# A bidirectional RWKV-7 / mLSTM trunk layer: the mLSTM scan in alternating half steps, gate rows computed in the RWKV scan, merge gates in half products, and a fixed TensorE order

## The chip, the cores and the metric

The kernel runs on one core of a Trainium2 chip, as one program. The core has five engines that run side by side: TensorE (PE in the profile; its weight loads are listed apart as PEld), VectorE (DVE), ScalarE (ACT), GpSimd (POOL) and SyncE (SP, which only issues DMAs here). The metric is device time in microseconds, the median of several runs. Everything is computed in float32; large matrix products are made of three products of rounded parts (see below).

## The reference

One layer on 128 context tokens and 1024 latent tokens, width 1024. The latent tokens start each directional scan from a given state; the context tokens start from zero and their final states are outputs.

```python
h = rmsnorm(x, norm_g[0]) * (1 + sc1) + sh1            # sc, sh, g from SiLU(cond) @ ada_w
z_r, z_m, z_g = split(h @ w_in)                        # 1920, 2064 and 2048 columns
y_r, S = rwkv7_bidir(centred_shift(z_r, mu), S0, ...)  # 8 heads of 64, two directions
y_m, (C, n, m) = mlstm_bidir(z_m, C0, n0, m0, ...)     # 4 heads of 128, two directions
gate_r, gate_m = split(sigmoid(z_g))
merged = gate_r * (y_r @ w_branch_rwkv) + gate_m * (y_m @ w_branch_mlstm)
x = x + g1 * rmsnorm(merged @ w_out, norm_g[1])
x = x + g2 * rmsnorm(conv_ffn(rmsnorm(x, norm_g[2]) * (1 + sc2) + sh2), norm_g[3])
```

The mLSTM, for one direction and head, over chunks of tokens (i, f are the log gates; b the running sum of f in the chunk; m the running maximum that keeps the exponentials small):

```python
log_d = where(mask, b[:, None] - b[None, :] + i[None, :], -inf)
m_s   = max(b + m, max(log_d, -1));  inter = exp(b + m - m_s)
s     = (q @ k.T) * exp(log_d - m_s)
num   = inter * (q @ C.T) + s @ v;   den = inter * (q @ n) + sum(s, -1)
h     = num / max(|den|, exp(-m_s))
m_new = max(b[-1] + m, max(b[-1] - b + i));  wj = exp(b[-1] - b + i - m_new)
C, n, m = decay * C + (wj * v).T @ k,  decay * n + wj @ k,  m_new
```

Then the two directions' h are added, normalised per head, scaled and multiplied by sigmoid(o).

## The kernel before

**Layout.** 1152 tokens are nine blocks of 128; block 0 is the context. The normalised input lies transposed in SBUF as AS, three groups of 384 tokens, each as a rounded part and a remainder. `split_w` (L334) loads a weight block, rounds it on ScalarE (L348) and takes the remainder on VectorE (L349); a product is the sum of three products of parts (`mm_split`, L357, its matmul L362).

**Stages in the source.** (1) Modulation, norm and the input projection with everything that prepares the RWKV scan. Its results (KRd, BKd, Vd, Ad ...) and the mLSTM's q, k, v, o and gate columns (qkd, vmd, sod, gtd) go to DRAM. (2) The RWKV scan, 18 steps of 64 tokens (`ORDER`); step n handles one chunk of each direction. (3) The mLSTM, one context chunk and eight latent chunks of 128 tokens in each direction. (4) The merge: branch products, gates (as tanh of half the argument), output projection. (5) The ConvFFN.

**The order within an engine** is not the source's order. The framework takes the source as a list, plans it with a model of the engines' times, and puts each engine's instructions in the order in which they become ready in that plan; dependencies become semaphore waits. An engine works its list in order. Buffers come from rings: the n-th tile of a tag waits until the tile that had its buffer is released.

**The RWKV scan.** `back` (L861) does step n: pP (L867), read out as Pm; pU (L874) into suv; pN (L882) into sn and the next step's suv; pY (L894, L895) into ysum. Between these it calls `between(n)` (L954), which does the next step's scores (`scores`, L813: psc L819, transposes pbk L822, masks L829 and L831), the merge of inverse blocks (`merge`, L836: pmh L843, pmt L852) and `fill(1)`. The loads of the next step (`loads`, L791: KA, BKs, TT on SP, XN on POOL) and of suv (`new_suv`, L761, on POOL) are issued at the step's start. Steps 0 and 1 are the context; after step 1 `finish_ctx` (L906) writes the final states (pfs L910) and `init_state` (L773) loads the latent ones (pst L783), all through the one buffer of tag sn2. `rpost(b)` (L918) finishes an output block: row statistics (L927 to L936), transposes into pgt (L942), pgg (L950), and the store to yrd; `POST` says after which step.

**Filler.** The gate columns z_g are sixteen blocks of 128 columns, each three groups of 24 matmuls (12 weight-part and k steps are one half). Four blocks lie in the preparation, blocks 4 to 12 are cut into groups by `zg_groups` (L710) and handed out by `fill`: one group per scan step, three in the last step, the rest (`fill(len(zq))`) written behind the mLSTM. Blocks 13 to 15 (`zg(f, pss)`) are written after that, next to the reloading of the branch inputs. Each block ends in a Tanh and a store to sgz.

**The mLSTM.** After the scan, three more `rpost`; then the gate rows: loads of gtd, exponentials, two scans along the tokens per direction, a small exchange through DRAM (red, mpd) for the running maximum over chunks, then Ms, it, dc stored to DRAM and three transposes (gT). `mchunk(d, c, CN)` does one chunk in full: it loads qk and vx and broadcasts of the rows (MI), forms dm in four VectorE operations (L1121), takes Exp (L1123), scales the query part of MI (L1124), forms the scores pmP (L1127) and multiplies them in (L1128), transposes k (pmk L1131), scales it (kw L1134), scales the state (CN2, POOL, L1136), and for each pair of heads pmN (L1143, L1144), den (three operations), hsum, pmC (L1161) and the new state (L1162). The two directions alternate. `mfinish(c)` normalises a chunk whose two directions are done (L1170 to L1179), transposes it (pmf L1184), multiplies by the output gate and stores to ymd; it is written one chunk late. After the context chunk the states go out (co, no) and the latent states come in (cn, nr), through the same tag sqm.

**The reload.** `load_y` (L1246) reads yrd and ymd back through the stage buffers (tag zraw, three of them) and splits them into y2r and y2m (L1250, L1251) for the branch products pbr.

## Time and profile before

| what | us |
|---|---|
| median of 3 runs | 2271.1 |
| lowest, highest run | 2270.51, 2271.61 |
| profiled execution, whole | 2279.22 |
| its span in the profile | 2277.5 |
| scan step 0 to step 17 (first and last Pm) | 638.4, 922.9 |
| first pmN of the mLSTM | 985.2 |
| first pbr of the merge | 1177.5 |
| TensorE clock granted, mean | 0.977 |

Times inside the profile count from the span's start. In rows of windows, the bracket behind a busy time is the number of instructions; in rows of groups, the two numbers behind the bar are total busy us and mean ns of one, then the idle time of the engine ahead of them with what ended it. A timeline row is start, length, engine, line, operation, out<-in, shapes and count; idle time ahead of it stands in square brackets.

### The profile page before, as it was taken

The page shows a single profiled execution, that of the slowest core. Times are in us where ns is not written, and L with a number is a line of the kernel's source. Part 1 is how long each engine was busy: PE and PEld are TensorE (multiplying, and loading weights), DVE is VectorE, ACT ScalarE, POOL GpSimd, SP SyncE. Part 2 cuts the span into 40 slices and gives each one's busy share as a digit, 9 for nine tenths or more (in the row PEclk, how much of TensorE's full clock was granted, in tenths as well). Part 3 has the DMA queues.
Part 4 walks back from the last instruction along what each step waited for, and adds up shares of the span by engine and source line. Part 5 has one row for each costly group of instructions (what it writes and reads, how often), then busy time and mean ns, then how long its engine had stood idle before and what let it go on. Part 6 is the DMA issues. An engine that isn't in the chain of part 4 may idle for free. (4 is left out here: it accounts for less than half of the span.)

```text
span 2277.5 us, 40164 instructions
## 1 busy us (share of the span) xinstructions
PE 2119.8 (93%) x16395; PEld 1945.6 (85%) x16395; DVE 1404.3 (62%) x2310; ACT 832.8 (37%) x1683; POOL 534.6 (23%) x699
## 2 busy tenths in 40 slices
PE   6999998989899998977789999999999999999996
PEld 4998997988878987877688978999999999999995
DVE  3766778879555566546833375736555655576558
ACT  3664646462143445434331143432222222222213
POOL 2000198888622233222302212000000000000004
PEclk9999999999989999989999999999999999999999
DMA  9134444545745655367666542111111111111104
GB/s 263 53 86 123 116 127 109 149 106 135 184 121 139 154 145 135 101 185 216 190 184 206 171 157 84 56 47 47 56 49 45 47 56 53 41 47 56 47 19 166
DMA packets 391416, 254.59 MB, mean 112 GB/s; under 512 B 86305, under 2 KB 368069, under 8 KB 391232
## 3 DMA queue, kind: packets, MB, share of 16 engines
q1 hardware_dynamic: 246864, 144.88, 22.7%
q10 hardware_dynamic: 135840, 88.03, 13.0%
q0 software_dynamic: 8528, 19.10, 3.2%
q8 instruction: 129, 2.11, 0.4%
q14 instruction: 55, 0.45, 0.1%
HBM read 186.73 MB, written 65.23 MB: 111 GB/s over the span
## 5 line engine op out<-in xcount | busy, mean ns | idle before, releaser
L362 PE MATMUL pg<-act,whi 128*128 128x384 f32 x4240 | 816.7, 339 | 4.5 <-ACT zraw L522 4.0
L362 PEld LDWEIGHTS pg<-act,whi 128*128 128x128 f32 x4240 | 740.1, 188 | 19.9 <-ACT zraw L522 4.3
L362 PE MATMUL pg<-act,wlo 128*128 128x384 f32 x2120 | 418.0, 337 | 5.0 <-DVE wlo L349 5.0
L362 PEld LDWEIGHTS pg<-act,wlo 128*128 128x128 f32 x2120 | 371.2, 188 | 8.7 <-DVE wlo L349 5.3
L349 DVE TENSOR_TENSOR wlo<-wraw,whi 128x1024 fp32r<-128x1024 f32 x130 | 164.1, 1264 | 226.6 <-ACT whi L348 226.4
L47 DVE SCALAR_TENSOR_TENSOR ua<-uraw,par,ua 128x945 f32<-128x945 f32 (+2 forms) x176 | 214.6, 1219 | 42.5 <-ACT ua L1392 39.3
L362 PE MATMUL pfd<-whi,f 128*128 128x512 f32 x792 | 227.5, 395 | 6.5 <-DVE facc L1464 6.5
L1466 POOL TENSOR_TENSOR x<-facc,grow 128x512 f32<-128x512 f32 x17 | 24.3, 1454 | 822.7 <-DVE facc L1464 822.7
L348 ACT ACTIVATE whi<-wraw 128x1024 fp32r<-128x1024 f32 x130 | 136.7, 1054 | 173.9 <-PE pg L362 99.6
L362 PEld LDWEIGHTS pfd<-whi,f 128*128 128x128 f32 x792 | 146.4, 188 | 37.2 <-DVE facc L1464 9.1
L1464 DVE TENSOR_TENSOR facc<-pfd,facc 128x512 f32<-128x512 f32 x180 | 121.9, 685 | 52.2 <-PE pfd L362 52.2
L509 POOL TENSOR_TENSOR Lb<-Lb,tmp 96x31 f32<-96x31 f32 (+15 forms) x155 | 130.6, 843 | 12.2
L507 POOL TENSOR_TENSOR tmp<-La,Lb 96x31 f32<-96x31 f32 (+15 forms) x155 | 122.6, 791 | 27.3 <-DMA La<-Ad 15.5
L362 PE MATMUL pfd<-wlo,f 128*128 128x512 f32 x396 | 122.6, 391 | 0.0
L1396 ACT ACTIVATE ua<-ua 128x1152 f32<-128x1152 f32 x22 | 25.7, 1168 | 221.3 <-DVE ua L47 221.2
L1406 ACT ACTIVATE f<-ua 128x384 fp32r<-128x384 f32 x66 | 32.1, 518 | 194.0 <-DVE ua L1405 194.0
L829 DVE TENSOR_TENSOR KA<-psc,msk 64x512 f32<-64x512 f32 x72 | 49.2, 684 | 70.2 <-ACT A L828 68.8
L47 DVE SCALAR_TENSOR_TENSOR qacc<-zraw,par,qacc 128x945 f32<-128x945 f32 (+2 forms) x64 | 85.9, 1342 | 9.3 <-ACT qacc L565 8.8
L1340 PE MATMUL pwo<-whi,act 128*128 128x512 f32 x288 | 90.2, 393 | 1.1 <-ACT whi L348 1.1
L362 PEld LDWEIGHTS pfd<-wlo,f 128*128 128x128 f32 x396 | 74.3, 188 | 16.8
L769 POOL DMA_DIRECT2D suv<-Vd x72 | 42.4, 599 | 152.5 <-DVE sn L887 81.8
L1405 DVE TENSOR_TENSOR ua<-pg,ua 128x384 f32<-128x384 f32 x66 | 34.5, 553 | 69.0 <-PE pg L362 53.4
(383 smaller groups left out, 3227.2 us busy)
## 6 DMA issues: line engine op xcount, KB each, us to landing
wraw<-in_w_in ACTq DMA_DIRECT2D x44, 512.0 KB
wraw<-in_ffn_up ACTq DMA_DIRECT2D x44, 512.0 KB
zraw<-in_ada_w SPq DMA_DIRECT2D x24, 512.0 KB
wraw<-in_ffn_down ACTq DMA_DIRECT2D x22, 512.0 KB
KRd<-KR SPq DMA_DIRECT2D x24, 384.0 KB
sgz<-zraw ACTq DMA_DIRECT2D x16, 576.0 KB
KA<-KRd SPq DMA_DIRECT2D x72, 128.0 KB
BKs<-BKd SPq DMA_DIRECT2D x36, 256.0 KB
```

Of the source, the lines that this page charges most:

```text
L47: v.scalar_tensor_tensor(o, img[:, r0 + i:r1 + i, c0 + j:c1 + j], wt, o, op0=ALU.mult, op1=ALU.add)
L348: s.activation(hi, raw, AF.Copy)
L349: v.tensor_tensor(lo, raw, hi.bitcast(F32), op=ALU.subtract)
L362: pe.matmul(out, wt(hw, k), at(ha, k), start=(i == 0), stop=(i == last))
L507: e.tensor_tensor(t3, L[:, j, i].unsqueeze(2).to_broadcast([NI, n, m]), X[:, j:j + 1, c].to_broadcast([NI, n, m]), op=ALU.mult)
L509: e.tensor_tensor(X[:, i, c], X[:, i, c], t3, op=ALU.subtract)
L769: pdma(suv[r, d, h].rearrange("t x p n -> t x (p n)"), src.unsqueeze(1).to_broadcast([64, 2, 4 * LC]))
L829: v.tensor_tensor(q.KA[orr, :, h, :], sc_[h][orr], msk[orr, d:d + 1, :].to_broadcast([64, 4, 128]), op=ALU.mult)
L1340: pe.matmul(pts[b][q], AS[g][:, ha, k, 128 * o:128 * o + 128], wo2[k][hw][:, 0, 512 * q:512 * q + 512], start=(k == 0 and i == 0), stop=(k ...
L1405: v.tensor_tensor(ua[:, gs], pt, ua[:, gs], op=ALU.mult)
L1406: s.activation(f2[:, 0, gs], ua[:, gs], AF.Copy)
L1464: v.tensor_tensor(acc[:, b, qs], pt, acc[:, b, qs], op=ALU.add)
```

## The change

Six edits, made together.

1. **Order.** `pe` becomes a wrapper. While its switch is on (from the first scan step to the end of the mLSTM), every matmul and transpose is pinned behind the TensorE instruction that was written before it.
2. **Halves.** `zg_groups` becomes a generator that stops after 12 of a group's 24 matmuls and after each group; `fill(n)` takes n halves. All of blocks 4 to 15 go through it. The stage ring has two buffers from the scan to the mLSTM's end and three again after it.
3. **Output blocks.** `rpost` is a generator in two parts, statistics first; the second part runs a step later, between the second direction's scores and pN. Six of the blocks come in steps 11 to 16; blocks 1 and 8 come after the scan with two halves each.
4. **Gate rows.** They move into a generator `gates` of six parts, one per scan step 3 to 8. The factor 128^-0.5 is folded into them.
5. **mLSTM.** `mchunk` is cut into `mload` (three half steps ahead), `mfront` (two ahead) and `mback`. The mask is added on POOL and the offset enters Exp as a bias, one per head; the scores of a chunk are formed once, kept as S and used by both directions; the query part is scaled on POOL; pmN and pmC hold four heads, and den, the state update and hsum are done for all four. PSUM is divided anew.
6. **The loop.** Each half step is mback, parts of two finishes, the front two ahead, and one half of a gate product. The context's states go out and the latent ones come in after the second half step, followed by two halves.

```diff
+    class Ordered:
+        on = False
+        def matmul(self, *a, **k):
+            return self.keep(nc.tensor.matmul(*a, **k))
...
+        def keep(self, i):
+            return tc.keep_in_program_order(i) if self.on else i
+    pe = Ordered()
...
+            for g in range(3):
+                if g == 1 and i + 1 < len(fs):
+                    load(fs[i + 1])
+                pt = psg([128, G3])
+                ops = [(h, k) for h in PARTS for k in range(8)]
+                for n, ((hw, ha), k) in enumerate(ops):
+                    pe.matmul(pt, w2s[f][hw][:, k, :], AS[g][:, ha, k, :], start=(n == 0), stop=(n == 23))
+                    if n == 11:
+                        yield
                 s.activation(sg[:, G3 * g:G3 * g + G3], pt, AF.Tanh, scale=0.5)
+                if g == 2:
+                    adma(sgz[f], sg)
+                yield
     def fill(n):
         for _ in range(n):
-            if zq:
-                i, f, g, run = zq.pop(0)
-                run(i, f, g)
+            next(zq, None)
...
+    zsc.close()
+    zst[0] = pool("zst2", 2, zsc)
...
             scores(n + 1, d, qs[d])
+            if d == 1 and posts:
+                next(posts.pop())
             yield
         m = merge(qs)
         next(m)
-        fill(1)
+        fill(2)
         next(m)
         yield
-    POST = {1: 0, 13: 4, 14: 5, 15: 3, 16: 6, 17: 2}
-    zq = zg_groups(list(range(NZ0, 16 - NZ1)))
+    POST = {1: 0, 11: 4, 12: 5, 13: 3, 14: 6, 15: 2, 16: 7}
+    zq = zg_groups(list(range(NZ0, 16)))
...
+        if 2 < n < 9:
+            next(gate)
         if n in POST:
-            rpost(POST[n])
+            posts.append(rpost(POST[n]))
+            next(posts[-1])
+    for b in (1, 8):
+        r = rpost(b)
+        next(r)
+        fill(2)
+        next(r)
...
+    banks(pg=2, ps=2, pf=2)
+    def mfront(q):
+        d, c = q.d, q.c
+        dm, qi = q.MI[:, 0], q.MI[:, 1]
+        q.vx = mp.tile([128, 4, 130], F32, name="vx", tag="vx", bufs=3)
+        dma(q.vx[:, :, 0:128], vmd[c])
+        gp.memset(q.vx[:, :, 128:129], 1.0)
+        gp.tensor_tensor(dm, dm, mbig[:, d:d + 1, :].to_broadcast([128, 4, 128]), op=ALU.add)
+        for h in range(4):
+            s.activation(dm[:, h, :], dm[:, h, :], AF.Exp, scale=-1.0, bias=cols(gT[0], d, c)[:, h:h + 1])
+        if c not in Ss:
+            pp_ = psf([128, 4, 128], "pmP")
             for h in range(4):
+                pe.matmul(pp_[:, h, :], q.qk[:, 4 + h, :], q.qk[:, h, :], start=True, stop=True)
+            Ss[c] = mp.tile([128, 4, 128], F32, name="S", tag="S", bufs=8)
+            s.activation(Ss[c], pp_, AF.Copy)
...
+        v.tensor_tensor(dm, Ss[c], dm, op=ALU.mult)
+        gp.tensor_tensor(qi, q.qk[:, 0:4, :], qi, op=ALU.mult)
...
+    CNs = state(False)
+    qs = [mload(*dc) for dc in SEQ[0:3]]
+    for q in qs[0:2]:
+        mfront(q)
+    fins, half = [], []
+    for i, (d, c) in enumerate(SEQ):
+        if i + 3 < len(SEQ):
+            qs.append(mload(*SEQ[i + 3]))
+        done = c in seen
+        CNs[d] = mback(qs[i], CNs[d])
+        for m in half:
+            next(m)
+        half = fins[0:1]
+        del fins[0:1]
+        for m in half:
+            next(m)
+        if i + 2 < len(SEQ):
+            mfront(qs[i + 2])
+        fill(1)
+        if done:
+            fins.append(mfinish(c))
+        if i == 1:
+            states_out(CNs)
+            CNs = state(True)
+            fill(2)
+    for m in half:
+        next(m)
+    for m in fins:
+        next(m)
+        fill(4)
+        next(m)
+    pe.on = False
...
+    mpc.close()
+    zsc.close()
+    zst[0] = pool("zst3", 3, zsc)
...
         load_y(ys[0], yrd, pdma)
-        for f in range(16 - NZ1, 16):
-            zg(f, pss)
+        fill(80)
         load_y(ys[1], ymd, dma)
```

More of the change, by code (lines that the diff above doesn't have):

```diff
@@ L329, in stage @@
     def stage():
[L330 removed]
+        return zst[0].tile([128, T], F32, name="zraw", tag="zraw")
     nsplit = [0]
@@ L954, in between @@
     def between(n):
         if n + 1 == len(ORDER):
-            for _ in range(3):
-                fill(1)
+            for i in range(3):
+                if i == 1 and posts:
+                    next(posts.pop())
+                fill(2)
                 yield
@@ L963, in between @@
             scores(n + 1, d, qs[d])
+            if d == 1 and posts:
+                next(posts.pop())
             yield
@@ L979, in _body @@
     init_state(False, suv)
+    gate = gates()
+    posts = []
+    pe.on = True
     for n in range(len(ORDER)):
@@ L1085, in _body @@
-    for t_, o in zip((gg, em, wj), gT):
-        pt = pss([128, 128], "pgt")
-        pe.transpose(pt, t_, ident)
-        v.tensor_copy(o, pt)
-    dma(decb, dcd.rearrange("d r -> (d r)").unsqueeze(0).to_broadcast([128, 72]))
     if stop == "yr":
@@ new lines, in state @@
+    def state(latent):
+        CNs = []
+        for d in range(2):
+            CN = mp.tile([128, 4, 130], F32, name="CN", tag=f"CN{d}")
+            if not latent:
+                gp.memset(CN, 0.0)
+            else:
+                cn = mf.tile([128, 4, 128], F32, name="cn0", tag="sqm")
+                dma(cn, A["state_mlstm_C"][0, 0, d].rearrange("h v k -> v h k"))
+                nr = mf.tile([4, 128], F32, name="nr0", tag="nr0")
+                dma(nr, A["state_mlstm_n"][0, 0, d])
+                pt = psf([128, 4, 128], "pmi")
+                for h in range(4):
+                    pe.transpose(pt[:, h, :], cn[:, h, :], ident)
+                v.tensor_copy(CN[:, :, 0:128], pt)
+                pt = psf([128, 4], "pmi2")
+                pe.transpose(pt, nr, ident[0:4, 0:4])
+                v.tensor_copy(CN[:, :, 128], pt)
+            CNs.append(CN)
+        return CNs
@@ new lines, in _body @@
+    MORD = [(0, 0)] + [(1 + i, 8 - i) for i in range(8)]
+    SEQ = [(d, cc[d]) for cc in MORD for d in range(2)]
+    CNs = state(False)
[22 more added lines that the diff above has]
+            CNs = state(True)
+            fill(2)
```

430 lines of the change are left out of this document (203 added, 227 removed).

## The prediction, made before the change was run

> **What bounds the kernel now.** I read the page first, then busy time by stage, then TensorE's waits in the stages that the change rewrites. From part 1 of the page:
>
> ```profile
> span 2277.5 us, 40164 instructions
> PE 2119.8 (93%) x16395; PEld 1945.6 (85%) x16395; DVE 1404.3 (62%) x2310; ACT 832.8 (37%) x1683; POOL 534.6 (23%) x699
> ```
>
> TensorE is the bound overall, but 93% is a mean. The stretch that the change touches, in six windows (columns: window, length, then busy time and instructions of PE, PEld, DVE, ACT, POOL, then PE clock, DMA share, GB/s):
>
> ```profile
> 638.00:923.00 285.00, 269.40 (x5142) 240.80 (x5139) 168.64 (x326) 130.35 (x396) 88.01 (x137) 0.98 0.52 132
> 923.00:985.00 62.00, 53.49 (x495) 47.34 (x494) 25.61 (x75) 28.00 (x78) 11.93 (x20) 0.94 0.43 119
> 985.00:1013.00 28.00, 19.69 (x122) 18.00 (x122) 15.35 (x45) 7.46 (x24) 6.50 (x9) 0.83 0.82 260
> 1013.00:1060.00 47.00, 38.18 (x286) 36.49 (x286) 27.50 (x108) 19.50 (x62) 10.60 (x16) 0.92 0.64 190
> 1060.00:1132.00 72.00, 50.69 (x334) 45.00 (x334) 62.38 (x204) 26.59 (x101) 27.63 (x37) 0.88 0.66 197
> 1132.00:1178.00 46.00, 40.35 (x222) 38.89 (x221) 16.92 (x28) 15.56 (x27) 2.42 (x3) 0.96 0.51 164
> ```
>
> They are the RWKV scan; its last step with the gate rows and three output blocks; the mLSTM context chunk and the state load; eight latent half steps; the other eight with the finishing; and the last gate products. Up to 923 and from 1132 TensorE has little room. In the 147 us between 985 and 1132 it is busy 108.6 us, at a granted clock of 0.83 to 0.92, and in 1060 to 1132 VectorE is busy 62.4 of 72 us: there it is the bound. TensorE's longest waits in 1060 to 1141 (columns: total, times, longest) say so:
>
> ```profile
> PE pmf L1184 <- DVE hsum L1179: 12.9, 14, 2.7
> PE pmN L1143 <- DVE dm L1128: 7.4, 6, 1.4
> ```
>
> The work that could lie there is the merge-gate products. TensorE's matmuls into pg by stage (first number in brackets):
>
> ```profile
> 638.40:690.90 52.50, 12.73 (x56) 10.13 (x56) 0.00 (x0) 1.45 (x3) 0.87 0.48 124
> 690.90:712.60 21.70, 5.64 (x23) 3.78 (x23) 0.00 (x0) 0.49 (x1) 1.00 0.46 115
> 712.60:845.20 132.60, 40.53 (x216) 37.01 (x216) 0.00 (x0) 4.42 (x9) 1.00 0.61 152
> 845.20:922.90 77.70, 18.48 (x97) 16.57 (x98) 0.00 (x0) 1.94 (x4) 1.00 0.42 108
> ...
> 1013.20:1132.00 118.80, 6.79 (x29) 4.79 (x29) 0.00 (x0) 1.01 (x2) 0.90 0.65 194
> ```
>
> The edges are the starts of scan steps 0, 2, 4, 13 and 17, then the start of the first latent chunk and the end of the last. Nine plain scan steps hold 24 each and take 132.6/9 = 14.7 us; the latent chunks hold 29 in 118.8 us.
>
> **The change, stage by stage.** Prices on TensorE, from one chunk's scores and from two groups of 24 gate matmuls in a row (start, length, instruction):
>
> ```profile
> 967.75 1.16 PE L1127 MATMUL pmP<-qk 128*128 128x128 f32 x8 [0.57 <-DVE yt L951]
> ...
> 1160.10 2.93 PE L362 MATMUL ps<-act,whi 128*128 128x384 f32 x16
> ...
> 1164.26 2.07 PE L362 MATMUL ps<-act,whi 128*128 128x384 f32 x11
> ```
>
> A group is 1164.26 - 1160.10 = 4.16 us, a half 2.08 us, one matmul 0.173 us. A float32 product is two records of about 0.12 us. Sharing the scores drops 9 x 8 records, 8.6 us; with the order fixed I find it again in the step lengths.
>
> *Scan, steps 0 to 16: 284.5 us before.* Between context and latent tokens lies a chain through one buffer: state out twice, state in twice.
>
> ```profile
> 662.79 1.15 PE L910 MATMUL pfs<-ident,sn 64*64 64x64 f32 x32
> 688.16 0.68 PE L783 MATMUL pst<-ident,st 64*64 64x64 f32 x16 [0.92 <-DMA st<-in_state_rwkv]
> ```
>
> It takes 25 us. The planner filled it with gate matmuls, an output block and the next scores, so steps 2 and 3 took only 21.7 us. In the fixed order all of that stands behind the second pst. Steps 2 and 3 then cost two plain steps and an output block, 2 x 14.7 + 3.2 = 32.6: **+10.9 us**. Step 0 holds 24 gate matmuls, where the order before left 17 of them for later: +2.9. An output block (rpost) costs TensorE 2.2 us, 32 records like pfs's and 8 like those of the scores; in steps 13 to 16 it cost 77.7/4 - 14.7 = 4.7, because its row statistics hold ScalarE and VectorE while scores wait to be read out (means, the third column behind the bar being idle time):
>
> ```profile
> L932 ACT ACTIVATE sqy<-ysum,ymu 128x64 f32<-128x64 f32 x72 | 25.0, 347 | 15.1 <-DVE ymu L928 7.4 <-DVE mpv L1053 5.7 <-ACT sqy L932 0.4
> ...
> L936 DVE TENSOR_SCALAR ysum<-ysum,ymu,yva 128x64 f32<-128x64 f32 x72 | 19.2, 340 | 15.2 <-POOL yva L934 15.1
> L934 POOL TENSOR_TENSOR yva<-yva,mhalf 128x8 f32<-128x8 f32 x9 | 15.0, 1666 | 23.8 <-DVE yva L933 23.8
> ...
> L932 ACT ACTIVATION_READ_ACCUMULATOR sqy<-ysum,ymu 128x1 f32 x72 | 13.6, 188 | 0.0
> ```
>
> Cut in two, the statistics, 8 x (0.35 + 0.19) + 1.7 + 8 x 0.34 = 8.7 us, run under the step's filler and merge and the next step's pP, pU and scores, about 11 of its 14.7 us. I leave 1 us of stall: 3.2 each (ends 2.2 and 4.7). Four in steps 13 to 16: -6; one more in step 12: +3.2. The gate rows in steps 3 to 8 bring SP about 25 issues, among them a load that waits for its own store, and ScalarE two or three table loads:
>
> ```profile
> 964.89 0.24 SPq L1060 DMA_DIRECT2D mpd<-mpv  x1
> ...
> 968.29 0.82 SPq L1064 DMA_DIRECT2D mc<-mpd  x2
> ```
>
> ```profile
> L1022 ACT ACT_TABLE_LOAD x1 | 1.3, 1283 | 0.0
> ```
>
> That is 3.4 us from store to load; queued behind it on SP are the KA loads, for which the next scores wait. I take +5 (ends 0, all beside filler, and 12: three waits of 3.4 and two of 1.3, rounded down). Stage: +2.9 + 10.9 - 6 + 3.2 + 5 = **+16**.
>
> *Step 17 to the first pmN: 62.3 us before.* After: three filler pairs 12.5, step and block 6.4, then block 1 (4.2 filler, 2.6 wait for its statistics, 2.2), block 8 (4.2 + 2.2), scores 1.8, and a wait. The first pmN needs on POOL mbig, two CN memsets that reuse rpost's buffers, an add and a product, then four Exp and a VectorE product: 7 us (ends 2 and 12: two POOL products, and all of them behind the last block's store). Together 43: **-19**. Most of that is the gate rows' chain, which no longer ends here: the first dm waited for the rows that it stores.
>
> ```profile
> 982.53 1.14 DVE L1121 SCALAR_TENSOR_TENSOR dm<-MI,gT,mbig 128x128 f32<-128x128 f32 x4 [7.46 <-DMA MI<-Mrd]
> ```
>
> *To the first latent pmN: 28 us before.* Two half steps of 6.4 = 12.8; states out 1.2; then the chain below, with no filler in front of it, since fill(2) is written behind state(True):
>
> ```profile
> 998.39 0.46 SPq L1226 DMA_DIRECT2D s_C<-co  x1
> ...
> 1009.04 1.09 PE L1204 MATMUL pmi<-ident,cn 128*128 128x128 f32 x4 [4.90 <-DMA cn<-in_state_mlstm_C]
> ...
> 1012.02 1.05 PE L1204 MATMUL pmi<-ident,cn 128*128 128x128 f32 x4
> ```
>
> That is 13.6 us from the store. Two large loads shared the DMA engines then and now come later, so I take 10 (ends 7 and 14); 2 us for the clock, 0.83 in this window before; 1.3 for pmi and 4.2 for fill(2): 31.5, **+3.5**.
>
> ```profile
> 999.57 1.17 POOL L1249 DMA_DIRECT2D zraw<-yrd  x2
> ```
>
> *Sixteen latent half steps: 118.8 us before.* TensorE per half step: pmN 1.9, pmC 0.95, transposes 0.5, half a gate product 2.08, and scores 0.95 (first eight) or the finish's transposes 0.5: 6.4 and 5.9 us. VectorE loses four dm operations and the query product and joins den and CN for two head pairs; POOL gains two products of 128x512. Its prices (mean ns behind the comma):
>
> ```profile
> L1136 POOL TENSOR_TENSOR CN<-CN,decb 128x516 f32<-128x516 f32 x18 | 19.9, 1106 | 31.9 <-DMA decb<-dcd 13.9 <-DVE CN L1208 10.3 <-DVE den L1147 2.5
> L947 POOL TENSOR_TENSOR yt<-yt,bon 128x512 f32<-128x512 f32 x9 | 11.6, 1289 | 36.4 <-ACT yt L946 36.4
> L1177 POOL TENSOR_TENSOR va<-va,mhalf 128x4 f32<-128x4 f32 x8 | 9.4, 1180 | 26.2 <-DVE den L1148 16.9 <-DMA qk<-qkd 9.2
> L1179 DVE TENSOR_SCALAR hsum<-hsum,mu,va 128x128 f32<-128x128 f32 x30 | 15.9, 564 | 1.8 <-POOL va L1177 1.8
> ```
>
> In the second eight POOL has 1.1 + 3 x 1.3 + 1.2 = 6.2 us per half step. VectorE's 62.4 us were some 7.5 a half step; less the five operations that leave it (four took 1.14 in the row above) under 6. So all engines are near 6. I take 6.6 for the first eight, 7.5 for six and 6 for the last two, which prepare nothing: 52.8 + 45 + 12 = 110, **-9** (ends: 5.9 and 9 for the six). L1179 takes 0.28 us each with POOL idle, against 0.56 on average:
>
> ```profile
> 1138.16 1.12 DVE L1179 TENSOR_SCALAR hsum<-hsum,mu,va 128x128 f32<-128x128 f32 x4 [1.20 <-POOL va L1177]
> ```
>
> [...]
>
> *From there to the first branch product: 45.6 us before.* It was covered by most of the window's 222 matmuls; now only fill(4), 8.3 us, and four leftover halves are there. The mLSTM output must go to DRAM, come back and be split. One such load, of yrd, before:
>
> ```profile
> 1148.53 0.64 POOL L1249 DMA_DIRECT2D zraw<-yrd  x1 [10.41 <-DVE y2r L1251]
> ...
> 1152.75 1.17 ACT L1250 ACTIVATE y2r<-zraw 128x1152 fp32r<-128x1152 f32 x1 [1.96 <-DMA zraw<-yrd]
> ```
>
> From issue to use 576 KB take 4.2 us; four take 11 at 210 GB/s (the windows above moved 190 to 260). After: 8.3, 2.3 for the last transposes and VectorE, 3.4 for the store as for mpd, 11, and 2.5 for the split, less 6.2 (36 matmuls) for y2r products that run meanwhile: 21.3, **-24.3**.
>
> **Sum:** 16 - 19 + 3.5 - 9 - 24.3 = -33 us. On the profiled execution (span 2277.5, 2279.2 us with what lies around it) that gives 2246; it ran 8 us above the median, so on the median 2271.1 it is 2238.
>
> **Rivals.**
> 1. *Both reloads open* (0.21): the stage buffers of y2r lie on those of the unfinished last gate block and of hsum, so yrd's loads also start only after the leftover halves. For: 3 buffers, 8 loads. Against: before, three of the four came early. Four more loads, part covered: +14, 2252.
> 2. *TensorE stays the bound* (0.17): six half steps at 5.9 (-10), no wait at the start (-5), no stall by blocks and gate rows (-8): 2215.
> 3. *Slower by the fixed order in the scan* (0.11): each step's scores wait for KA loads, 0.68 us in this step already, and with more issues on SP ahead of the loads no filler may overtake the wait.
>
> ```profile
> 801.59 1.13 PE L819 MATMUL psc<-KA,BKs 64*128 64x128 f32 x14 [0.68 <-DMA KA<-KRd]
> ```
>
> Over 16 steps 2.1 us each cancels the gain; at 3 us, +48, 2286. Against: plain steps already ran almost in this order.
> 4. *No change* (0.07): fillers only move, and the chains and the tail pay back all of it: 2271.
>
> **How the numbers follow.** The forecast has 0.44: 2238, its own range 2222 to 2256. Eight in ten: low end, rival 2 with the state wait at 7 and a little more, 2208; high end, rival 1 with the six half steps at 9 and gate rows at 12, 2252 + 9 + 7, and part of rival 4: 2271. Faster by over 0.2% (what a measurement of this kernel can tell from no change): 0.44 + 0.21 + 0.17 = 0.82; within 0.2%: 0.07; slower: 0.11.
>
> **What would show it.** Scan steps 2 and 3 at over 30 us together, with TensorE idle ahead of pst, show the chain; plain steps over 15.5 us show rival 3. The first pmN should come about 3 us earlier than 985, pmi should end an idle gap of 8 to 14 us, half steps should be 6 to 8 us apart with POOL or VectorE the last releaser, and y2m's split should end TensorE's wait ahead of pbr; y2r there speaks for rival 1. I am wrong altogether if the latent half steps take 9 us with the filler inside them, or if the steps of the scan grow.

## The result and the profile after

The changed kernel takes 2310.73 us (median of 4 runs, 2308.44 to 2311.24), the kernel before 2271.36 us on the same chip (4 runs, 2270.51 to 2273.31): a ratio of 1.017, with a 95% interval of 1.0153 to 1.0188. It is slower by 1.7%; the forecast was 2238 us. The profiled execution took 2310.34 us, its span is 2308.6 us. The kernel before was profiled in an execution of 2279.22 us, 8 us above its median, so the traces show 31 of the 39 us. From part 1 of the page after:

```profile
PE 2109.4 (91%) x16323; PEld 1944.2 (84%) x16323; DVE 1361.5 (59%) x2140; ACT 847.8 (37%) x1746; POOL 572.8 (25%) x725
```

TensorE is busy 10 us less than before and the span is 31 us longer, so its idle time grew by some 41 us. Where, the windows of the changed kernel say; the edges are the starts of scan steps 0, 4, 12 and 17, the first pmN, the first latent pmN, the last half step's pmC, and the first branch product pbr:

```profile
600.00:654.00 54.00, 37.50 (x295) 35.88 (x294) 16.54 (x44) 11.56 (x27) 14.73 (x30) 0.78 0.72 153
654.00:738.80 84.80, 67.61 (x1258) 61.57 (x1260) 38.76 (x73) 28.59 (x83) 21.12 (x34) 0.84 0.47 115
738.80:861.20 122.40, 118.05 (x2323) 106.93 (x2323) 69.31 (x119) 50.30 (x136) 36.24 (x64) 0.99 0.57 138
861.20:967.80 106.60, 89.72 (x1629) 81.26 (x1626) 62.91 (x143) 53.15 (x182) 32.30 (x39) 0.89 0.46 115
967.80:1027.10 59.30, 39.79 (x385) 37.16 (x384) 15.59 (x36) 22.01 (x72) 18.06 (x21) 0.81 0.43 128
1027.10:1057.70 30.60, 24.42 (x139) 23.06 (x140) 11.33 (x26) 11.81 (x39) 12.97 (x13) 0.75 0.60 182
1057.70:1164.40 106.70, 94.45 (x688) 91.09 (x687) 55.57 (x147) 56.42 (x201) 60.44 (x64) 0.97 0.69 204
1164.40:1201.10 36.70, 23.75 (x131) 22.40 (x129) 11.83 (x37) 9.05 (x24) 5.33 (x7) 0.83 0.57 191
```

Two columns matter. Length less PE busy is TensorE's idle time, 16.9 us of 106.6 in the fourth row. The third number from the end is its granted clock: 0.89 there, where the kernel before had 1.00:

```profile
831.10:922.90 91.80, 83.46 (x1597) 74.70 (x1594) 61.35 (x138) 51.83 (x180) 30.43 (x38) 1.00 0.47 120
```

For an estimate of what the clock takes I worked out for each half microsecond what its PE busy time times the missing share of the clock gives, and summed it. Both kernels, stage by stage, in us; the latent half steps end at the start of the last pmC in both:

| stage | before: length, idle, lost to the clock | after |
|---|---|---|
| last products ahead of the scan, from 600 | 38.4, 4.0, 1.5 | 54.0, 16.5, 4.6 |
| scan steps 0 to 3 | 74.2, 4.8, 6.8 | 84.8, 17.2, 6.7 |
| scan steps 4 to 11 | 118.5, 2.5, 0.0 | 122.4, 4.4, 1.7 |
| scan steps 12 to 16 | 91.8, 8.3, 0.0 | 106.6, 16.9, 8.9 |
| step 17 to the first pmN | 62.3, 8.7, 2.9 | 59.3, 19.5, 5.4 |
| to the first latent pmN | 28.0, 8.1, 3.5 | 30.6, 6.2, 5.6 |
| latent half steps | 114.5, 29.0, 10.7 | 106.7, 12.2, 3.4 |
| to the first pbr | 49.8, 6.8, 1.7 | 36.7, 12.9, 1.7 |
| sum | 577.5, 72.2, 27.1 | 601.1, 105.8, 38.0 |

The latent half steps brought what was forecast. Idle time there fell by 17 us, and by 2 us in the stage ahead of them; in the six others it rose, by some 52 us in sum. The loss to the clock rose by 10.9 us over all eight. The 23.6 us lost up to the first pbr become 31.0 at the last (1309.8 before, 1340.8 after), since the first pbr groups still wait for y2r (4.8 us more) and run at a lower clock: from the first pbr to the last the same estimate gives 6.9 us lost to it, against 3.4 before. What the idle time waits for, from TensorE's waits in five stretches of the changed kernel (steps 0 to 3, steps 12 to 16, the start of the mLSTM, the tail; total, times, longest):

```profile
PE pst L81 <- DMA st<-in_state_rwkv: 13.7, 2, 11.4
...
PE pgt L81 <- DVE AB L853: 8.1, 5, 4.6
...
PE pmP L81 <- issue: 8.3, 1, 8.3
PE pgt L81 <- DVE ysum L958: 4.8, 2, 3.8
PE pmN L81 <- DMA vx<-vmd: 4.5, 1, 4.5
PE pmk L84 <- ACT S L1190: 2.0, 1, 2.0
...
PE pbr L81 <- ACT y2r L1344: 15.6, 4, 10.8
```

None of these is a matmul waiting for a matmul. Each is a load, a store or another engine's work that the order before had covered with gate products; for pmP the profile names nothing, and a run below shows what it waited for. The pgt of steps 12 to 16, the transposes of the output blocks, do not wait for the blocks' statistics. From step 12:

```profile
867.17 1.88 DVE L958 TENSOR_SCALAR ysum<-ysum,ymu,yva 128x64 f32<-128x64 f32 x8 [1.79 <-POOL yva L956]
...
869.77 0.42 DVE L853 TENSOR_TENSOR AB<-psc,msk 64x256 f32<-64x256 f32 x1
...
870.33 1.98 PE L81 MATMUL pgt<-ident,ysum 64*64 64x64 f32 x32 [4.56 <-DVE AB L853]
```

The statistics end with L958 at 869.05. The transposes start at 870.33, 0.14 us behind the mask AB of the second direction's scores, and so do the other four. In the source pgt takes the next of three PSUM buffers (ring pf; TensorE's products go there) behind the two psc and the pbk of these scores, which is the buffer of the first psc; it comes free when VectorE has masked that psc, and the masks stood on VectorE behind L958. So the statistics hold the transposes only through VectorE's order. No run gives pgt a buffer of its own.

And ahead of the scan stands one that my sum does not have. The timeline there, from the first direction's scores to the second's:

```profile
628.37 1.16 PE L81 MATMUL psc<-KA,BKs 64*128 64x128 f32 x16
...
629.47 0.66 PE L84 MATMUL pbk<-ident,BKs 128*128 128x128 f32 x4
633.73 1.27 SPq L1016 DMA_DIRECT2D rr<-red  x2
635.00 0.20 DVE L1026 TENSOR_SCALAR mm<-rr 4x1 f32<-4x1 f32 x1 [17.93 <-DMA rr<-red]
...
639.42 0.16 DVE L1044 TENSOR_TENSOR mx<-mc,bG 128x1 f32<-128x1 f32 x1 [2.88 <-DMA mc<-mpd]
...
639.87 0.40 ACT L1055 ACTIVATE gf<-GG,mcs 128x128 f32<-128x128 f32 x1 [12.67 <-DVE mcs L1053]
...
642.80 0.56 ACT L850 ACTIVATE A<-psc 32x128 f32<-32x128 f32 x2 [0.91 <-DMA dcd<-dc]
...
644.03 2.67 PE L81 MATMUL psc<-KA,BKs 64*128 64x128 f32 x16 [13.91 <-ACT BT L856]
```

Lines 1016 to 1063 are the gate rows, written in scan steps 3 to 8. They run here, ahead of step 0: only TensorE's order is fixed, and the planner put them on VectorE, ScalarE and SyncE as early as their inputs allowed. VectorE then stood 17.9 us at a row's load (rr) that waits for its own store, ScalarE 12.7 us behind VectorE, and the scores' read-out (L850) behind both, so TensorE waited 13.9 us.

### The profile page after: what moved, and what is told of

It is laid out like the page before. It is cut to its first block, busy times and chain, and to the rows that moved or that the text cites. A ratio compares the mean times of both kernels' runs of the same rounds, so it can differ in the third digit from the quotient of the medians.

```text
span 2308.6 us, 39893 instructions
## 1 busy us (share of the span) xinstructions
PE 2109.4 (91%) x16323; PEld 1944.2 (84%) x16323; DVE 1361.5 (59%) x2140; ACT 847.8 (37%) x1746; POOL 572.8 (25%) x725
## 3 DMA queue, kind: packets, MB, share of 16 engines
q10 hardware_dynamic: 135840, 88.03, 13.1%
## 5 line engine op out<-in xcount | busy, mean ns | idle before, releaser
L81 PE MATMUL pg<-act,whi 128*128 128x384 f32 (+1 forms) x4416 | 856.0, 341 | 8.6 <-ACT zraw L537 5.6
L81 PEld LDWEIGHTS pg<-act,whi 128*128 128x128 f32 (+1 forms) x4416 | 778.1, 190 | 24.4 <-ACT zraw L537 6.0
L81 PE MATMUL pg<-act,wlo 128*128 128x384 f32 (+1 forms) x2208 | 436.1, 337 | 7.7 <-DVE wlo L364 7.7
L81 PEld LDWEIGHTS pg<-act,wlo 128*128 128x128 f32 (+1 forms) x2208 | 388.0, 188 | 11.2 <-DVE wlo L364 8.0
L1559 POOL TENSOR_TENSOR x<-facc,grow 128x512 f32<-128x512 f32 x17 | 24.3, 1454 | 822.7 <-DVE facc L1557 822.7
```

The source lines that it names most:

```text
L81: return self.keep(nc.tensor.matmul(*a, **k))
```

## The experiments

Eighteen kernels, all the changed kernel with one or more edits. Times are medians; the ratio is to the kernel before, run on the same chip each time, so ratios compare across groups better than medians do.

### Is it the fixed order?

```diff
-    pe.on = True
+    pe.on = False
```

> The changed kernel with the one switch that fixes TensorE's order left off, so that all the rest of the change stays (half steps, shared scores, gate rows in the scan, split output blocks). Against the kernel before the changed one is 39.4 us later. Theory: most of that is not the fixed order itself, but work of other engines put ahead of what TensorE waits for (gate rows at the start of the scan, 15.6 us; two blocks' statistics in one step, 9 us) and waits for memory and stores (state chain 13.7 us, start of the mLSTM 20 us, reload 10.9 us). Gate products that move up again cover the state chain and part of the rest: 2285 us (2275 to 2298), with the wait ahead of the branch products still there. Rival 1, the fixed order is the whole loss: under 2265 us. Rival 2, the order costs nothing and the waits are there in any order: 2305 to 2315 us.

Measured: 2272.9 us, ratio 0.9996 (0.998 to 1.0013). Without the fixed order the rest of the change is worth nothing and costs nothing. That is below my range and above the rival's: the order is the whole loss, but not the whole list of waits. The first Pm came at 655.0 here too, against 638.4 before, and the tail's wait for y2r was 15.9 us as with the order fixed; what made up for them is that the waits at pst and at the start of the mLSTM were covered again.

Next the switch at the end of the scan:

```diff
-    pe.on = True
     for n in range(len(ORDER)):
...
     banks(pg=2, ps=2, pf=2)
+    pe.on = True
```

> The changed kernel with TensorE's order fixed from the mLSTM on and free in the scan. The kernel with a free order everywhere ran at 2272.9 us, the changed one at 2310.7. Theory: the fixed order costs in the scan and at its seams, where the waits for the state loads, gate rows and block statistics are met with nothing in front, and costs nothing in the latent half steps, where TensorE is fed evenly: 2273 us (2266 to 2280), the half steps 6.1 us apart as with the whole order fixed. Rival: the free order's gain lies in the mLSTM and the tail (its last gate products overtake the finishing): 2290 to 2305.

Measured: 2294.1 us, 1.0075 (1.0048 to 1.0102). The theory's number fell and the rival's range holds: by the ratios the order costs about as much from the mLSTM on (18 us above the free order) as in the scan (22 us below the changed kernel). The first eight half steps were mostly 6.1 us apart, as expected; what the order costs there lies at the seams, with waits of 9.4 us at pmP, 4.6 at the first pmN and 4.5 at pmi.

### One wait at a time

**State chain.** The latent states go into the output block's buffers:

```diff
-            st = cp.tile([128, 4, 64], F32, name="st0", tag="sn2", bufs=1)
+            st = rp.tile([128, 4, 64], F32, name="st0", tag=("yt", "bon")[d])
```

> The changed kernel with the two latent RWKV states loaded into the output block's two buffers, not yet in use, in place of the one buffer that the context state leaves last. TensorE's order is the same. Theory: the 13.7 us that pst waits for its loads go, and the matmuls behind it run at a higher clock: 2296 us (2292 to 2300), steps 1 and 2 together 40 us in place of 53.7. Rival, the wait moves to the next thing in the fixed order (the loads of keys for step 3 or output block 0's statistics): 2304 to 2311.

Measured: 2293.3 us, 1.008 (1.0054 to 1.0106). Step 1 fell from 32.5 to 17.5 us, step 2 went from 21.2 to 23.4: 40.9 in sum. TensorE's waits of steps 0 to 2 in that kernel hold no pst any more:

```profile
PE psc L81 <- DVE AB L853: 2.0, 1, 2.0
PE pgt L81 <- DVE AB L853: 1.6, 1, 1.6
PE pN L81 <- ACT suv L898: 1.2, 4, 0.3
PE pP L81 <- PE pst L81: 0.3, 1, 0.3
```

**Gate rows.** A wrapper holds each instruction of `gates` on VectorE, ScalarE and GpSimd behind what is written before it:

```diff
+    class Pinned:
+        def __init__(self, e):
+            self.e = e
+        def __getattr__(self, nm):
+            return lambda *a, **k: tc.keep_in_program_order(getattr(self.e, nm)(*a, **k))
+    pv, ps_, pp = Pinned(v), Pinned(s), Pinned(gp)
-        v.scalar_tensor_tensor(bb, gf, -1.0, gf, op0=ALU.mult, op1=ALU.max)
+        pv.scalar_tensor_tensor(bb, gf, -1.0, gf, op0=ALU.mult, op1=ALU.max)
...
```

> The changed kernel with the gate rows' instructions on VectorE, ScalarE and GpSimd held in the order in which they are written, that is, in scan steps 3 to 8. Theory: of the 15.6 us by which the scan starts later, 13.9 are TensorE's wait for score read-outs that stand on ScalarE and VectorE behind gate rows, and these behind loads of rows just stored; with the rows in their steps that wait goes and some 4 us come back in steps 3 to 8: 2299 us (2294 to 2304), first Pm near 640. Rival, the later start comes from the stage buffers (two in place of three) or from the gate products that are no longer moved ahead of the first scores: within 3 us of the changed kernel's 2310.7, first Pm still near 654.

Measured: 2307.1 us, 1.0135 (1.0102 to 1.0168). The first Pm came at 639.2, as the theory has it, so the planner's early placement is what delayed the scan. The time lies 3 us above the theory's range, for steps 5 and 8 grew to 20.3 and 23.7 us, from 15.1 and 17.9, and the last pbr came only 0.4 us earlier. From the timeline of step 8:

```profile
799.70 0.34 SPq L1084 DMA_DIRECT2D decb<-dcd  x1
...
803.10 1.29 SPq L831 DMA_DIRECT2D TT<-Xtd  x3
...
810.13 1.10 ACT L880 ACTIVATE TT<-pmt 32x128 f32<-32x128 f32 x4 [7.04 <-DMA TT<-Xtd]
...
811.62 0.48 PE L84 MATMUL pgt<-ident,gi 128*128 128x128 f32 x1 [8.15 <-ACT gi L987]
```

ScalarE waits 7.0 us for a step's late load, the rows' Exp stands behind it, and the fixed order lets no gate product pass the transpose of the rows (here named pgt too). The price of the rows in a fixed order was some 14 us in either place.

**Reload.** First the stage buffers are laid behind the y2 tiles, then y2m and y2r get a pool each:

```diff
-    zst[0] = pool("zst3", 3, zsc)
-    with tc.tile_pool(name="br", bufs=1) as bp, tc.tile_pool(name="brl", bufs=2) as bl:
+    with tc.tile_pool(name="br", bufs=1) as bp, tc.tile_pool(name="zst3", bufs=3) as z3, \
+            tc.tile_pool(name="brl", bufs=2) as bl:
+        zst[0] = z3
```

> The changed kernel with the tail's three stage buffers laid behind the two y2 tiles in place of on top of the last gate block's buffers. Theory: the loads of yrd no longer wait for the last gate block's store, so they run beside the leftover gate products; the 10.9 us wait ahead of the first branch product goes, and y2m, whose loads wait for the stage buffers of y2r, comes earlier too: 2297 us (2293 to 2301), first branch product at 1190 to 1194. Rival, what remains is y2m's own path, store of the last output block, load and split, which only starts at 1183: then the first product comes early but the stage ends within 4 us of now, 2306 to 2311.

Measured: 2308.1 us, 1.0143 (1.0119 to 1.0168); first pbr at 1197.3, last pbr 2.9 us earlier than in the changed kernel. The time is the rival's, but not its cause: the loads came early, yet the first split of y2r began 4.8 us after the last gate block's store had been issued, and y2m did not hold it:

```profile
1196.04 3.27 ACT L1345 ACTIVATE y2r<-zraw 128x1152 fp32r<-128x1152 f32 x3 [4.78 <-DMA wraw<-in_w_branch_mlstm]
```

I took it that y2r's tile does not lie on that block's buffers, while the pool that it shares with y2m does. The next edit asks that:

```diff
-    with tc.tile_pool(name="br", bufs=1) as bp, ...
+    with tc.tile_pool(name="brm", bufs=1) as bm, tc.tile_pool(name="brr", bufs=1) as br, ...
```

> The kernel early_reload again with the tiles of y2m and y2r in a pool each. There the loads of yrd came early, but the first split of y2r still began at 1196.0, when the last gate block's store had landed, since both tiles lay in one pool on top of that block's buffers. Theory: with y2r's tile in a pool of its own its splits run beside the last gate products, the first branch product starts at 1188 to 1192, and y2m's loads, which wait for the same stage buffers, some 8 us earlier: 2299 us (2295 to 2303). Rival: y2m, store of the last output block at 1183, load and split, is what ends the stage; then 2305 to 2309.

Measured: 2299.3 us, 1.0104 (1.0077 to 1.0132), as the theory has it. In the timeline of ScalarE the first split now begins 21 us earlier:

```profile
1174.91 1.17 ACT L1345 ACTIVATE y2r<-zraw 128x1152 fp32r<-128x1152 f32 x1 [6.35 <-DMA zraw<-yrd]
```

So the split had waited for what lay under the shared pool, and not under its own tile. The first pbr came at 1191.0, and TensorE's waits of the tail show the rival's wait right behind, which is why the last pbr gained 6.5 us and not 10:

```profile
PE pbr L81 <- ACT y2m L1345: 9.8, 1, 9.8
```

**Start of the mLSTM.** Four of the leftover halves are written ahead of the first scores:

```diff
     qs = [mload(*dc) for dc in SEQ[0:3]]
+    fill(4)
     for q in qs[0:2]:
         mfront(q)
```

> The changed kernel with four half gate products, of those left over for the tail, written ahead of the first scores of the mLSTM. Theory: TensorE idles 14.8 us there (8.3 for the loads held behind the last block's store, 2.0, 4.5), so four halves, 8.3 us, cost nothing there; the last gate block's store lands 8 us earlier and the loads of yrd with it: 2303 us (2300 to 2306). Rival: the tail only loses the cover of y2m's path: 2308 to 2312.

Measured: 2302.7 us, 1.0126 (1.0101 to 1.015), as the theory has it. And the cause of that idle time:

```diff
-    rp = pool("rpost", 1, rpc)
     ysp = pool("ysp", 1, rpc)
...
+    rp = pool("rpost", 1, rpc)
     gup = rp.tile([128, 512], F32, name="gup", bufs=1)
...
-    mbig = mf.tile([128, 2, 128], F32, name="mbig", bufs=1)
+    mbig = mp.tile([128, 2, 128], F32, name="mbig", tag="mbig", bufs=1)
```

> The changed kernel, order fixed, with the output blocks' buffers laid where no buffer of the mLSTM comes to lie, so that the mLSTM's first loads and memsets need not wait for the last block's store to land (in the changed kernel both start at 1012.5, just then, and TensorE waits 14.8 us between the last block's product at 1008.3 and pmN at 1027.1). Theory: the memory is what holds the loads; with it apart they land before the last block ends, and 9 to 13 us of the 14.8 go: 2299 us (2296 to 2302). Rival: SyncE's queue holds them, where the block's store waits ahead of them: 2308 to 2312.

Measured: 2298.1 us, 1.0096 (1.0065 to 1.0128), as the theory has it. It was the memory: SyncE issues the first loads of the mLSTM ahead of the last two blocks' stores now, and of the 14.8 us at pmP, pmk and pmN 1.9 are left, while the blocks' own wait for ysum rose from 4.8 to 10.0. SyncE's timeline in the changed kernel, then in this one, then TensorE's waits at that place:

```profile
997.60 12.91 SPq L975 DMA_DIRECT2D yrd<-yt  x2
1012.81 0.33 SPq L1167 DMA_DIRECT2D qk<-qkd  x1
```

```profile
980.78 0.33 SPq L1167 DMA_DIRECT2D qk<-qkd  x1
...
1001.41 12.81 SPq L975 DMA_DIRECT2D yrd<-yt  x2
```

```profile
PE pgt L81 <- DVE ysum L958: 10.0, 5, 4.4
PE pmP L81 <- DVE yt L974: 1.7, 1, 1.7
PE pmk L84 <- ACT S L1190: 0.2, 1, 0.2
```

### The split output blocks

**Statistics in their own step**, with the same wrapper around the first half of `rpost`:

```diff
-        v.tensor_reduce(mu, y, axis=mybir.AxisListType.X, op=ALU.add)
+        pv.tensor_reduce(mu, y, axis=mybir.AxisListType.X, op=ALU.add)
...
```

> The changed kernel with the output blocks' row statistics (means, squares, power, scaling) held behind what is written before them on their engines. In the changed kernel the statistics of blocks 4 and 5 ran together in step 12 (16 squares on ScalarE between the score read-outs), and the transposes of block 4 waited 4.6 us. Theory: two blocks' statistics in one step are what makes step 12 longer (23.0 us against 14.1 before): step 12 falls to 18 to 20, steps 13 to 16 stay near 21: 2307 us (2304 to 2309). Rival: a block's own statistics take longer than what the fixed order puts between its halves, whichever step they run in: all five steps stay at 20 to 23, 2309 to 2313.

Measured: 2331.0 us, 1.0252 (1.0224 to 1.0281), some 20 us slower than the changed kernel, against both lines. Steps 12 to 16 all took 24 us. The early statistics of block 5 in step 12 were thus no loss: with all of them held in their steps, every block's transposes wait over 4 us, for the mask AB again. Its waits and its window for steps 12 to 16:

```profile
PE pgt L81 <- DVE AB L853: 21.5, 5, 4.5
```

```profile
860.30:981.10 120.80, 94.84 (x1632) 85.97 (x1631) 60.91 (x136) 50.90 (x173) 30.80 (x38) 0.86 0.40 102
```

**More distance**: the second half waits in a list until the next block's first half has been written:

```diff
-            if d == 1 and posts:
-                next(posts.pop())
+            if d == 1 and len(posts) > (n > 3):
+                next(posts.pop(0))
...
-                    next(posts.pop())
+                    next(posts.pop(0))
...
+    for r in posts:
+        next(r)
     for b in (1, 8):
```

> The changed kernel with the second half of each output block (transposes, gate product, store) of steps 12 to 16 one step later, so that a whole step lies between a block's statistics and the transposes that need them; block 0's stays. TensorE's order stays fixed. With the statistics held in their own step the transposes waited 4.3 us in every one of these steps and a step took 24; in the changed kernel they take 19 to 23, and before the change 18 to 21. Theory: the fixed place of the transposes, too soon behind the statistics, is the cost: steps 12 to 17 lose 10 to 15 us, 2298 us (2295 to 2302), 17.5 to 18.5 each. Rival: the statistics' 16 us of ScalarE and VectorE work between the score read-outs is the cost, wherever the transposes stand: steps of 20 to 22, 2307 to 2313.

Measured: 2297.9 us, 1.011 (1.0088 to 1.0131): the expected time, but not for the expected reason. A step with a block still took 21.7 us on average (steps 13 to 16: 23.8, 22.8, 19.0, 21.4). Step 12, now without one, fell to 14.3, and the last block's transposes went behind the scan. In the profile 7.4 us of span were gained, not 12.8. The theory's step lengths fell. The transposes' waits went from 8.1 to 3.7 us only, and what releases them is still the mask: in step 13 they start at 884.16, while the block's statistics had ended at 879.05. The waits of the score matmuls for read-outs by VectorE and ScalarE stayed, 8.1 us in steps 12 to 16 against 7.1.

**Whole blocks**, at the steps of the kernel before, in a free order with the two edits below:

```diff
-    POST = {1: 0, 11: 4, 12: 5, 13: 3, 14: 6, 15: 2, 16: 7}
+    POST = {1: 0, 13: 4, 14: 5, 15: 3, 16: 6, 17: 2}
...
             next(posts[-1])
+            next(posts.pop())
-    for b in (1, 8):
+    for b in (7, 1, 8):
```

> The kernel free_order_reload_rows (2258.2 us) with the output blocks whole, at the steps of the kernel before (13 to 17, and three behind the scan). Theory: the split and the earlier places of the blocks are what lengthens the scan's last steps in a free order too (106 us against 92 before); whole, they take 92 to 96 again and one block goes back behind the scan for some 4: 2249 us (2245 to 2254). Rival: the steps are longer for their TensorE clock, lowered by waits of any kind, and stay long: 2256 to 2262.

Measured: 2250.6 us, 0.9882 (0.9859 to 0.9906), the time that the theory has, and the lowest of all medians (its interval overlaps that of free_order_reload_rows_blocks below). Steps 12 to 16 in a window of it, and below the same steps with split blocks (free_order_reload_rows):

```profile
843.80:936.80 93.00, 84.83 (x1597) 76.11 (x1593) 61.22 (x138) 51.81 (x179) 30.97 (x38) 0.98 0.45 118
```

```profile
843.30:943.00 99.70, 91.20 (x1629) 81.09 (x1626) 63.70 (x143) 52.92 (x182) 32.34 (x39) 0.95 0.48 123
```

6.7 us less, but not for fewer waits: TensorE is idle 8.2 us in the one and 8.5 in the other. By the sum used above the clock took 1.7 us in place of 4.7, and one block, some 2.2 us of TensorE, lies elsewhere. With split blocks the longest waits here are 6.3 us for KA loads, in three, which whole blocks do not have. So a wait for statistics is not what whole blocks saved in a free order. The first pbr came 14.3 us earlier (1139.0 against 1153.3), the last 7.6.

### Together

Two pools, order free; then with the gate rows' wrapper too, around their loads and stores as well:

> Free order and the reload in two pools together. With the free order alone TensorE still waited 10.9 us for the first split of y2r (15.9 with the three after it), as with the fixed one, where the two pools brought 11.4. Theory: the tail's wait comes from the memory layout and not from the order, so it goes here too: 2262 us (2258 to 2266), faster than before the change (2274.2 on that chip). Rival: in the free order no gate products are left for y2m's path and the wait moves there: 2269 to 2274.

> The same with the gate rows held in steps 3 to 8, their loads and stores on SyncE's queue too (in gate_rows_pinned these could move up and stood in front of the key loads, 8 us in step 8). Theory: the first step comes 14 us earlier, as it did there, and with a free order the steps that carry the rows can fill the waits with gate products, so that nearly all of it is kept: 2250 us (2246 to 2257). Rival: the rows take the same time from the steps that carry them, since ScalarE and VectorE run in the order planned whatever TensorE does: 2259 to 2265.

Measured: 2265.9 us, 0.9972 (0.9957 to 0.9987), and 2258.2 us, 0.9924 (0.9902 to 0.9947). Both beat the kernel before. The first came 4 us above its line, within its range, the second between its two lines; the rows brought 7.7 of the 13 us that step 0 came earlier, for steps 5 and 8 grew to 18.8 and 22.5 us.

The second halves a step later on top, then the block's buffers apart as well:

> The kernel free_order_reload_rows (2258.2 us) with the second halves of the output blocks a step later as well. Theory: in the free order, too, the steps with blocks ran at a granted clock of 0.90 and took 106 us in place of 92; a step of distance brings about what it brought in the fixed order, 8 to 12 us: 2248 us (2244 to 2252). Rival: with a free order the transposes move to where they can run anyway, and nothing changes: 2256 to 2261.

> The same with the output blocks' buffers apart as well. Theory: the free order already covers most of the mLSTM's start with gate products (its waits there sum to some 6 us), so the buffers bring little on top: 0 to 5 us less than the kernel without them, 2245 us (2242 to 2250). Rival: the later gate products now lack at the tail, and it is no faster or slower by up to 4 us.

Measured: 2253.4 us, 0.9907 (0.9879 to 0.9935), between the two lines; and 2260.3 us, 0.9936 (0.9912 to 0.9959), the rival's case, if a little beyond it. The intervals of these two and of free_order_reload_rows overlap, so nothing is to be read from their order.

With the order fixed, first states, two pools and the four halves; then the second halves a step later and the gate rows too; then the block's buffers apart:

> The changed kernel, order fixed, with three mendings together: own buffers for the states, the reload in two pools, four half gate products at the start of the mLSTM. Alone they brought 17.4, 11.4 and 8.0 us. Theory: each fills or removes a wait at a place of its own, so they add, less the 4 to 8 us that the last two share (both shorten the wait for the reload): 2276 us (2272 to 2282), level with before the change. Rival: in a fixed order a mended wait only shows the next one: 2285 to 2295.

> The kernel fixed_order_waits_mended (2278.7 us) with the second halves a step later (12.7 us alone) and the gate rows held in steps 3 to 8 with their loads and stores (in the free order these brought 7.7). Theory: they are at other places and add: 2260 us (2256 to 2266), now faster than before the change with the order still fixed. Rival: the gate rows' waits in steps 3 to 8 cannot be filled in a fixed order and take back what the earlier start gives: 2266 to 2272.

> The kernel fixed_order_five_mended (2271.3 us) with the output blocks' buffers apart, which alone brought 12.7 us. Theory: the wait at the start of the mLSTM is its own; the four half gate products already placed there cover some 8 of it, so 4 to 8 us are left to win: 2265 us (2260 to 2269), below the kernel before with the order still fixed. Rival: nothing is left there once the products cover it: 2269 to 2274.

Measured: 2278.7 us, 1.0024 (1.0012 to 1.0036); 2271.3 us, 0.9988 (0.9971 to 1.0005); 2262.0 us, 0.9932 (0.9911 to 0.9953). The first is as the theory has it, the second the rival's case (steps 5 and 8 took 18.6 and 23.8 us), the third a little better than the theory. With six waits mended the fixed order is as fast as free_order_all, 0.9932 against 0.9936, which has four of the six mendings: with these waits mended the order itself costs nothing that shows. In the changed kernel the order and the waits that it uncovers cost 38 us. A fixed order with whole blocks was not run.

The same sum as above, from 600 to the first pbr: six mended 555.6 us, with 69.1 idle and 28.2 lost to the clock; whole blocks in a free order 539.0, 54.4 and 19.2.

## Why the prediction was wrong

The direction was wrong, and the sum by 56 us at the first pbr: -33 forecast, +23.6 measured. Step by step:

- **What bounds the kernel**: right. There was room between 985 and 1132, and filling it paid: latent half steps 112.6 us from the first latent pmC to the last before, 104.7 after. The -9 forecast is -8 so measured: 6.2 us each in the first eight, where I had 6.6, and 8.0 in the six behind them (1109.6 to 1157.4), where I had 7.5. One reading was off without harm: VectorE's 62.4 us over eight half steps are 7.8 each, not 7.5, so what is left for it is about 6. Some VectorE operations took longer with one of POOL beside them: dm's product L1197 takes 0.69 us in the median and took 1.45 at 1113.08, with a POOL product running from 1112.71 to 1113.98, and the four of L1246 (the L1179 of before) took 1.84 us at 1052.90, where seven of their nine groups took 1.12, beside a POOL operation from 1052.84 to 1053.89. Few did, and no run tells what lengthened them, or how much of the 8.0 is due to it.
- **Scan, the state chain**: right in kind, and in size over the four steps. Steps 0 to 3 were forecast at +2.9 + 10.9, measured +10.6, with 13.7 us of idle at pst; the run with own buffers shows the chain. The split is less good: steps 2 and 3 grew by 13.5 us and steps 0 and 1 together became 2.9 shorter, so that the sum came out is in part luck.
- **Scan, gate rows (+5 in steps 3 to 8)**: the step that failed first. I took it that work runs where it is written. The change pins TensorE only; the rows ran ahead of step 0 and delayed it by 15.6 us, which is nowhere in my sum. Held in steps 3 to 8 they would have cost some 14, above my upper end of 12, as the SyncE waits that I had listed come out as waits of ScalarE.
- **Scan, output blocks (-6 in steps 13 to 16, +3.2 in step 12)**: mis-sized in sign, +5.9 and +8.9 measured. I set 8.7 us of statistics against 11 us of other work and allowed 1 us of stall. The transposes waited 8.1 us in five steps, and 8.9 went to the clock; the other idle time, 8.8, is about that of before. I priced a wait for statistics; what the transposes waited for was a PSUM buffer that VectorE had to read out first, behind statistics, and this was nowhere in my sum. Cutting the block brought nothing: whole blocks in a free order were no slower.
- **Step 17 to the first pmN (-19)**: -3. I priced the wait at 7 and named the cause in my upper end only, all of it behind the last block's store. The waits were 8.3 + 2.0 + 4.5 = 14.8, the blocks' 4.8 where I had 2.6, the clock 5.4 where I had nothing. The run with the buffers apart shows that memory held the loads.
- **To the first latent pmN (+3.5)**: +2.6. Less waiting than I took (4.6 at pmi), more clock.
- **Tail (-24.3)**: -13.1 from the last pmC on. This is rival 1, which I had priced at +14: both reloads were open and pbr waited 15.6 us for y2r. The two runs on the reload show why: the stage buffers lay on top of the last gate block, and so did the pool of y2r and y2m. I gave it a chance of 0.21 because three of four loads came early before; but they had done so in a layout that the change replaces.
- **Rival 3** had the right verdict with the wrong place. Steps 4 to 11 grew by 3.9 us in sum, 2.8 of it in step 8 with the rows' transposes; TensorE waited 0.4 us for KA loads there. The fixed order costs at seams, where a wait stands alone.

Most of the mistakes have one root. The -33 counted each idle stretch of the new order from the rows of the old one, where gate products covered what I priced at nothing or at its lower end, and I took the sum of five stages' likeliest values though their errors point the same way. My low price for waits left out the clock, which by the estimate above took 10.9 us more than before.

Two things stay open. Where a run gained (7.4 to 13.6 us of span in the runs on the states, the blocks' distance and their memory), its median gained 0.7 to 5.4 us more; I put that down to the spread between executions and did not settle it. And TensorE has 21 us less to do at full speed up to the first pbr, of which the shared scores explain 8.6; I did not take the rest apart.

## What to carry to other kernels

Before you fix one engine's order, list the waits that the free order covers (a chain through one buffer, a load behind its own store, a pool laid on another's last tile) and mend them first; fixed before that, they came out here with 13.7 us at pst and 14.8 at the start of the mLSTM. Pinning one engine does not pin the others: work written later in the program may be put ahead of what the pinned engine waits for (here VectorE then stood 17.9 us and ScalarE 12.7 us at gate rows, and TensorE 13.9 us behind both), so look at what stands in front of it on those engines, and at which read-out must free the shared buffer that its next product takes. Give tiles whose lifetimes differ pools of their own (11.4 us here for the reload), and lay the last-released buffer where nothing urgent comes next (12.7 us for the output blocks).

## What the runs showed of the hardware

I had not expected how much the clock takes. Windows of the changed kernel around the wait at 630 (first busy time is PE's, third number from the end its clock):

```profile
630.00:632.00 2.00, 0.12 (x2) 0.00 (x0) 0.00 (x0) 0.00 (x0) 0.00 (x0) 1.00 0.90 320
632.00:633.00 1.00, 0.00 (x0) 0.00 (x0) 0.00 (x0) 0.00 (x0) 0.00 (x0) 0.77 0.00 0
633.00:644.00 11.00, 0.00 (x0) 0.00 (x0) 3.81 (x14) 3.15 (x8) 0.00 (x0) 0.50 0.27 75
644.00:648.00 4.00, 3.71 (x20) 3.08 (x20) 2.61 (x6) 0.77 (x3) 0.00 (x0) 0.50 1.25 108
648.00:653.00 5.00, 3.67 (x96) 3.29 (x96) 0.77 (x2) 1.72 (x6) 2.19 (x4) 0.50 0.89 39
653.00:655.00 2.00, 0.31 (x2) 0.34 (x4) 0.00 (x0) 0.60 (x1) 0.00 (x0) 0.50 0.29 51
655.00:659.00 4.00, 4.00 (x42) 3.44 (x42) 1.82 (x4) 1.13 (x3) 0.00 (x0) 0.50 0.29 79
659.00:660.00 1.00, 1.00 (x18) 0.88 (x18) 0.40 (x2) 0.00 (x0) 0.00 (x0) 0.58 0.86 257
660.00:664.00 4.00, 4.00 (x105) 3.71 (x105) 2.97 (x6) 1.73 (x4) 0.00 (x0) 1.00 0.40 92
```

About 2.5 us after TensorE fell idle the clock was halved, from 1.00 to 0.50, and it stayed so for some 16 us after the wait had ended, through stretches in which TensorE was busy 3.7 of 4 and 3.7 of 5 us; here it came back behind 5.1 us without a pause (from 654.69). Sixteen score matmuls took 2.67 us at 644, at 0.50, against 1.16 at 628, at 1.00. In steps 12 to 16, with waits of up to 4.6 us, the clock was 0.89 in the mean, where the kernel before, with none there over 1.92, kept 1.00. What a return needs the traces leave open: at 915.5 the clock came back though TensorE had paused for 0.15 us (busy 3.35 of the 3.5 us before), and in the kernel before it stayed at 0.50 from 669 to 682 with TensorE busy for all of these 13 us by the trace. By the estimate in the table above the clock alone took 38.0 us of the changed kernel's stages, 10.9 more than before.
